# From expert 1 on, w_down is loaded by ScalarE's DMA queue and w_gate_up by SyncE's

## The chip, the core and the metric

The kernel runs on one core of a Trainium2 chip. The core has a matrix engine (TensorE, PE in the profile; its weight loads are PEld), VectorE (DVE), ScalarE (ACT), GpSimd (POOL) and SyncE (SP), each with its own stream of instructions that runs in order. DMA transfers are issued by SP, ACT or POOL and are carried by 16 DMA engines. The metric is the device time of one execution in microseconds, the median of several; less is better.

## The reference

One decoder layer on 512 tokens of 1024 float32 values: three token mixers, an output projection and a layer norm, and then the part that matters here, a routed mixture of 32 experts of which each token uses four:

```python
logits = (xt @ router_w + router_b).astype(F32)
top_val, top_idx = lax.top_k(logits, TOP_K)          # 4 of 32
gate = jax.nn.softmax(top_val, axis=-1)
...
gu = xb @ w_gu[e] + b_gu[e]                          # w_gu[e]: 1024 x 2048
glu = jnp.minimum(gu[:, :D_FF], SWIGLU_LIMIT)
lin = jnp.clip(gu[:, D_FF:], -SWIGLU_LIMIT, SWIGLU_LIMIT)
act = glu * jax.nn.sigmoid(SWIGLU_ALPHA * glu) * (lin + 1.0)
return act @ w_dn[e] + b_dn[e]                       # w_dn[e]: 1024 x 1024
```

The expert outputs are weighted with the gates, summed for each token, added to the layer's input and normalised. All weights are float32: 8 MB of w_gate_up and 4 MB of w_down for each expert, 403 MB (384 x 1 MB) in all.

## The kernel before

The mixers run first (until about 400 us); the experts follow, one after the other, in `experts` (L1348). What belongs to expert e is called g for w_gate_up and d for w_down in this section.

**Chunks and the ring.** Weights come in chunks of 1 MB, 128 partitions by 8 KB: eight chunks g.0 to g.7 for an expert (`load_gu`, L1175), each 128 rows of w_gate_up, and four chunks d.0 to d.3 (`load_dn`, L1183), each 256 rows of w_down. `chunk` (L1165) hands out slots of a ring of 18 in the order of the calls, so a chunk may be loaded when the chunk 18 calls earlier has been read by PE. `load` (L1170) issues the transfer. Before, all are issued by SyncE (`nc.sync`), so all go through one queue, q1 in the profile. Each of the eight DMA semaphores (DMAHW0 to DMAHW7 in the order's rows) is given to every eighth of these transfers, and an issue first waits until the semaphore's earlier transfer is in: no transfer goes out before the one eight places earlier has landed.

**An expert on PE.** At most 96 rows of an expert are done here. The low 64 rows always run: `gu_low` (L1264), per chunk g.k eight matmul records of L1268. The rows 65 to 96 are the optional half, `gu_high` (L1270, L1273), in two blocks of four chunks behind a branch on the expert's count of rows (`past64`, L1257); experts 0 and 31 run it without a branch. `swiglu` (L1275) works on DVE and ACT; `swiglu_T` (L1288) transposes its result on PE (L1295) and ACT copies it to the tile aT, of which there is one. `dn` (L1299) multiplies with w_down: low rows L1314, optional rows L1309 behind a branch. ACT evacuates (L1318: eo0 and eo1) and POOL scatters the rows with an accumulating DMA (L1319). In the loop, after the fourth chunk of an expert the loads of the next expert's w_gate_up and of its own w_down are called, its xg rows for two experts on are gathered by POOL (L1193), and the next expert's rows are transposed (L1207, copies L1208). `dn` of an expert runs behind the w_gate_up products of the next one. The instructions of each engine stand in an order that a scheduler chooses from these calls and from its own estimate of when each can run; it is fixed when the program is built.

**The tail.** `tail` (L1512) adds the last expert's rows by matmuls, and normalises.

Of the kernel before, what the change touches and what calls it, by code (L numbers as in the profile page):

```python
# [126 lines left out]
class Trunk:  # L127
# [1039 lines left out]
        self.nchunk += 1  # L1167
        return self.slot(tag, "wc", dt)[:, 0:2048], self.ring_ins if self.nchunk <= FIRST and tag != "r" else None

    def load(self, dst, src, gate):  # L1170
        i = self.nc.sync.dma_start(dst, src)
        if gate is not None:
            self.after(i, gate)

# [8 lines left out]
    def load_dn(self, e):  # L1183
        out = []
        for k in range(0, NK, 2):
            w, gate = self.chunk()
            self.load(w.rearrange("p (k c) -> p k c", k=2), self.a["w_down"][e, k * 128:(k + 2) * 128].rearrange("(p k) c -> p k c", k=2), gate)
            out += [w[:, 0:1024], w[:, 1024:2048]]
        return out

# [489 lines left out]
```

## Time and profile before

| | us |
|---|---|
| median of 3 runs | 1492.03 (1488.74 to 1493.71) |
| the profiled execution | 1492.41 |
| its span, first to last instruction | 1490.7 |
| first transfer of an expert's weights issued | 294 |
| expert 31: first and last w_gate_up product | 1408.47, 1431.4 |
| last w_down product | 1454.2 |

The profile records one execution. Its views: the page (busy shares, forty slices of the span, queues), busy time by stretch, who waited for whom, and time lines of single engines. A start in a time line is in us from the span's start; "x8" is a run of eight equal instructions and the second number is how long the run took. A busy PE is not a PE at its peak, since matmuls are pipelined and their ends are modelled.

### The profile page before, as it was taken

The numbers are of one execution on the slowest core, as the hardware profiler recorded it, in microseconds if no ns is written. First come the engines' busy times: TensorE is split into PE (matmuls) and PEld (weight loads), VectorE is DVE, ScalarE is ACT, GpSimd is POOL, SyncE is SP. The second block draws the span as 40 slices with busy tenths as digits, with TensorE's granted clock in tenths as the row PEclk, the third lists the DMA queues.
The fourth block names the chain that finished last, engine by engine and source line by source line (L and its number), as shares of the span: only waits on it lengthen the run. The fifth ranks groups of instructions, "written<-read, shape, count | busy, mean of one in ns | idle before, by whom it ended". The sixth has DMA issues, their size and how long they took to land. (4 is left out here: it accounts for less than half of the span.)

```text
span 1490.7 us, 19988 instructions
## 1 busy us (share of the span) xinstructions
PE 1345.4 (90%) x7852; PEld 639.2 (43%) x7853; DVE 466.6 (31%) x1108; ACT 290.7 (20%) x611; POOL 228.2 (15%) x206
## 2 busy tenths in 40 slices
PE   7899989998899999988799999999879888899993
PEld 5677888876533433232233333333323222333322
DVE  4867497697831212111111111111111110211115
ACT  4444243353211111111001111111100110111103
POOL 1111137142301010001001111011100100010111
PEclk9999888799899999999999999999999999999996
DMA  7222123355689999999999999999999999999964
GB/s 250 70 57 71 36 68 89 118 159 205 256 341 396 393 383 404 402 398 390 395 399 398 394 398 399 402 395 391 392 387 398 395 401 394 404 396 412 401 223 127
DMA packets 95232, 461.67 MB, mean 310 GB/s; under 512 B 18137, under 2 KB 26745, under 8 KB 45962
## 3 DMA queue, kind: packets, MB, share of 16 engines
q1 hardware_dynamic: 79674, 434.57, 74.1%
q0 software_dynamic: 10880, 21.32, 6.6%
q10 hardware_dynamic: 4560, 4.15, 0.9%
q8 instruction: 82, 1.34, 0.4%
q14 instruction: 36, 0.29, 0.1%
HBM read 445.97 MB, written 18.10 MB: 311 GB/s over the span
## 5 line engine op out<-in xcount | busy, mean ns | idle before, releaser
L1268 PE MATMUL gu<-wc,xT 128*64 128x512 f32 x2048 | 486.6, 606 | 67.0 <-DMA wc<-w_gate_up 64.4
L1268 PEld LDWEIGHTS gu<-wc,xT 128*64 128x64 f32 x2048 | 143.0, 138 | 392.9 <-issue 239.5
L1281 DVE TENSOR_SCALAR glu<-gu 128x256 f32<-128x256 f32 (+1 forms) x64 | 35.6, 556 | 843.8 <-PE gu L1273 391.5
L1314 PE MATMUL dn<-wc,aT 128*64 128x512 f32 x1024 | 247.6, 603 | 4.2 <-PEq L1261 2.4
L1282 ACT ACTIVATE glu<-glu 128x256 f32<-128x256 f32 (+1 forms) x64 | 33.6, 525 | 549.6 <-DVE glu L1281 549.4
L1193 POOL DMA_INDIRECT xg<-hd,gidx x31 | 31.3, 1009 | 665.0 <-PE tr L1207 659.7
L1314 PEld LDWEIGHTS dn<-wc,aT 128*64 128x64 f32 x1024 | 65.8, 136 | 117.6 <-issue 101.3
L1319 POOL DMA_INDIRECT yd<-eo,sidx x45 | 70.1, 1557 | 276.1 <-ACT eo L1318 276.1
L1273 PE MATMUL gu<-wc,xT 128*32 128x512 f32 x960 | 111.3, 596 | 0.0
L222 PE MATMUL pi<-xhi,whi 128*128 128x512 f32 x152 | 63.7, 419 | 8.9 <-ACT whi L172 8.9
L1208 ACT ACTIVATE xT<-tr 128x384 f32<-128x384 f32 x62 | 29.9, 490 | 177.2 <-PE tr L1207 177.2
L223 PE MATMUL pi<-xlo,whi 128*128 128x512 f32 x152 | 62.8, 413 | 0.6 <-DVE xlo L173 0.6
L1273 PEld LDWEIGHTS gu<-wc,xT 128*32 128x32 f32 x960 | 27.7, 109 | 79.3 <-issue 79.3
L224 PE MATMUL pi<-xhi,wlo 128*128 128x512 f32 x152 | 61.7, 406 | 0.0
L173 POOL TENSOR_TENSOR wlo<-wraw,whi 128x512 fp32r<-128x512 f32 (+1 forms) x28 | 39.3, 1407 | 134.9 <-ACT whi L172 129.4
L1318 ACT ACTIVATE eo<-dn,gate 128x512 f32<-128x512 f32 (+1 forms) x45 | 28.0, 621 | 162.9 <-PE dn L1314 84.4
L1309 PE MATMUL dn<-wc,aT 128*32 128x256 f32 x960 | 56.1, 381 | 1.0 <-ACT aT L1296 1.0
L172 ACT ACTIVATE whi<-wraw 128x512 fp32r<-128x512 f32 (+1 forms) x54 | 33.9, 631 | 56.4 <-DMA wraw<-w_in 25.3
L1309 PEld LDWEIGHTS dn<-wc,aT 128*32 128x32 f32 x960 | 29.5, 110 | 33.3 <-issue 13.8
L1284 DVE SCALAR_TENSOR_TENSOR glu<-glu 128x256 f32<-128x256 f32 (+1 forms) x64 | 35.6, 556 | 8.4 <-ACT glu L1282 7.1
L1295 PEld LDWEIGHTS tr<-ident,glu 128*128 128x128 f32 x192 | 25.7, 208 | 28.0 <-DVE sel L1214 19.5
L222 PEld LDWEIGHTS pi<-xhi,whi 128*128 128x128 f32 x152 | 29.5, 194 | 18.2 <-ACT whi L172 8.6
(489 smaller groups left out, 1585.8 us busy)
## 6 DMA issues: line engine op xcount, KB each, us to landing
wc<-w_gate_up SPq DMA_DIRECT2D x256, 1024.0 KB
wc<-w_down SPq DMA_DIRECT2D x128, 1024.0 KB
wraw<-w_in SPq DMA_DIRECT2D x46, 256.0 KB
wraw<-w_out SPq DMA_DIRECT2D x16, 256.0 KB
xraw<-xT SPq DMA_DIRECT2D x4, 512.0 KB
res<-x SPq DMA_DIRECT2D x4, 512.0 KB
hd<-res ACTq DMA_DIRECT2D x4, 512.0 KB
res<-yd POOLq DMA_DIRECT2D x4, 512.0 KB
```

The source lines that it names most:

```text
L172: self.hi_ins = nc.scalar.activation(hi, src, AF.Copy)
L173: return (eng or nc.vector).tensor_tensor(lo, src, hi, OP.subtract)
L222: nc.tensor.matmul(p, hi, xh, start=(k == 0), stop=False)
L223: nc.tensor.matmul(p, hi, xl, start=False, stop=False)
L224: nc.tensor.matmul(p, lo, xh, start=False, stop=(k == NK - 1))
L1268: mm(p[q][64 * h:64 * h + 64], xT[:, k, 0:64], w[:, 1024 * q + 512 * h:1024 * q + 512 * h + 512], start=False, stop=(k == NK - 1))
L1273: self.nc.tensor.matmul(p[2][32 * c:32 * c + 32], xT[:, k, 64:96], w4[:, c], start=False, stop=(k == NK - 1), skip_group_check=True)
L1281: nc.vector.tensor_scalar(out[:, c], g, 7.0, None, OP.min)
L1284: nc.vector.scalar_tensor_tensor(out[:, c], ln[:, c], 1.0, out[:, c], OP.add, OP.mult)
L1309: mm(p2[32 * c:32 * c + 32], aT[:, 4 + k % 2, 32 * (k // 2):32 * (k // 2) + 32], wd[k][:, 256 * c:256 * c + 256], start=(k == 0), stop=(k ...
L1314: mm(p0[64 * h:64 * h + 64], aT[:, k % 4, 64 * (k // 4):64 * (k // 4) + 64], wd[k][:, 512 * h:512 * h + 512], start=(k == 0), stop=(k == N ...
L1319: return nc.gpsimd.indirect_dma_start(out=self.yd.rearrange("t (c f) -> (t c) f", f=w), out_offset=bass.IndirectOffsetOnAxis(ap=self.sidx[ ...
```

## The change

`load` takes the issuing engine as an argument, and `load_dn` hands it ScalarE for every expert but 0. So 124 of the 384 transfers are issued by ACT's stream, between its activations, and go through ACT's queue (q10). Slots, sizes and semaphores stay as they are; the eight semaphores now go round over the transfers of both queues in the order that the scheduler gave them.

```diff
-    def load(self, dst, src, gate):
-        i = self.nc.sync.dma_start(dst, src)
+    def load(self, dst, src, gate, eng=None):
+        i = (eng or self.nc.sync).dma_start(dst, src)
...
-            self.load(w.rearrange("p (k c) -> p k c", k=2), self.a["w_down"][e, k * 128:(k + 2) * 128].rearrange("(p k) c -> p k c", k=2), gate)
+            self.load(w.rearrange("p (k c) -> p k c", k=2), self.a["w_down"][e, k * 128:(k + 2) * 128].rearrange("(p k) c -> p k c", k=2), gate, self.nc.scalar if e else None)
```

The change also moves the scheduler's order. ACT in the middle, before, one round: sigmoids of expert 27 (glu_9063), transposed rows of expert 29 (xT_9213), outputs of expert 26 (eo0_9091, eo1_9127), transposed result of expert 27 (aT_9130):

```order
L1282 ACTIVATE glu_9063<-glu_9063 128x256
L1282 ACTIVATE glu_9063<-glu_9063 128x512
L1208 ACTIVATE xT_9213<-tr_9214 128x384
L1208 ACTIVATE xT_9213<-tr_9220 128x384
L1261 COMPARE_AND_BRANCH
L1318 ACTIVATE eo1_9127<-dn2_3901,gate_3575 128x256
L1261 UNCONDITIONAL_BRANCH x2
L1318 ACTIVATE eo0_9091<-dn0_9074,gate_3575 128x512
L1296 ACTIVATE aT_9130<-tr_9131 128x512
L1296 ACTIVATE aT_9130<-tr_9137 128x256
```

After, the round that begins behind aT_9130. wc_9204, wc_9206 and wc_9208 are d.1, d.2 and d.3 of expert 28, wc_9003 is d.0 of expert 27, which PE reads behind expert 28's w_gate_up, and eo1_9326 is expert 27's output:

```order
L1171 DMA wc_9204<-w_down 128x2048
L1171 DMA wc_9003<-w_down 128x2048
L1208 ACTIVATE xT_9213<-tr_9214 128x384
L1208 ACTIVATE xT_9213<-tr_9220 128x384
L1261 COMPARE_AND_BRANCH
L1261 UNCONDITIONAL_BRANCH x2
L1171 DMA wc_9206<-w_down 128x2048
L1261 COMPARE_AND_BRANCH
L1318 ACTIVATE eo1_9326<-dn2_3901,gate_3575 128x256
L1261 UNCONDITIONAL_BRANCH x2
L1171 DMA wc_9208<-w_down 128x2048
```

Behind these come the sigmoids of expert 28, eo0 of 27 and the aT copies of 28. Four issues now stand between ACT's copies and sigmoids, wc_9003 behind wc_9204; by the slot that it takes, wc_9204 waits for PE's products with g.3 of expert 28. The copies to xT_9213 have moved from ahead of aT_9130 to behind it.

SyncE at the end, before: g.4 to g.7 of expert 31 (wc_9592 to wc_9598), d.0 to d.3 of expert 30 (wc_9600 to wc_9606), the first of expert 31 (wc_9774; wc_9776, wc_9778 and wc_9780 follow), with the semaphores that each waits for:

```order
L1171 DMA wc_9592<-w_gate_up 128x2048 [waits DMAHW5_49,PE_49]
L1171 DMA wc_9594<-w_gate_up 128x2048 [waits DMAHW6_49,PE_49]
L1171 DMA wc_9596<-w_gate_up 128x2048 [waits DMAHW7_49,PE_49]
L1171 DMA wc_9598<-w_gate_up 128x2048 [waits DMAHW0_49,PE_49]
L1171 DMA wc_9600<-w_down 128x2048 [waits DMAHW1_49]
L1171 DMA wc_9602<-w_down 128x2048 [waits DMAHW2_49,PE_49]
L1171 DMA wc_9604<-w_down 128x2048 [waits DMAHW3_49,PE_49]
L1171 DMA wc_9606<-w_down 128x2048 [waits DMAHW4_49,PE_49]
L1171 DMA wc_9774<-w_down 128x2048 [waits DMAHW5_49,PE_49]
```

SyncE there after; nothing follows of the weights:

```order
L1171 DMA wc_9590<-w_gate_up 128x2048 [waits DMAHW7_49,PE_49]
L1171 DMA wc_9592<-w_gate_up 128x2048 [waits DMAHW1_49,PE_49]
L1171 DMA wc_9594<-w_gate_up 128x2048 [waits DMAHW3_49,PE_49]
L1171 DMA wc_9596<-w_gate_up 128x2048 [waits DMAHW6_49,DMAHW5_49,PE_49]
L1171 DMA wc_9598<-w_gate_up 128x2048 [waits DMAHW6_49,DMAHW0_49,PE_49]
```

ACT there after, behind its issue of wc_9606 (aT_9724 and glu_9657 are expert 30's, xT_9608 is 31's):

```order
L1208 ACTIVATE xT_9608<-tr_9609 128x384
L1208 ACTIVATE xT_9608<-tr_9615 128x384
L1282 ACTIVATE glu_9657<-glu_9657 128x512
L1282 ACTIVATE glu_9657<-glu_9657 128x256
L1171 DMA wc_9776<-w_down 128x2048
L1318 ACTIVATE eo0_9685<-dn0_9668,gate_3575 128x512
L1296 ACTIVATE aT_9724<-tr_9725 128x512
L1296 ACTIVATE aT_9724<-tr_9731 128x256
L1171 DMA wc_9778<-w_down 128x2048
L1171 DMA wc_9780<-w_down 128x2048
L1171 DMA wc_9600<-w_down 128x2048
L1171 DMA wc_9774<-w_down 128x2048
```

The eight w_down chunks that stood behind wc_9598 are now on ACT, and in the order over both engines all but wc_9600 and wc_9774 stand ahead of wc_9598, which by its semaphore waits for wc_9606.

PE at the end, before: low and optional products (gu2) of g.6 and g.7 of expert 31 in turn, then w_down of expert 30 and the transposes:

```order
L1268 MATMUL gu0_9735<-wc_9596,xT_9608 64x512 x2
L1268 MATMUL gu1_9736<-wc_9596,xT_9608 64x512 x2
L1273 MATMUL gu2_9737<-wc_9596,xT_9608 32x512 x4
L1268 MATMUL gu0_9735<-wc_9598,xT_9608 64x512 x2
L1268 MATMUL gu1_9736<-wc_9598,xT_9608 64x512 x2
L1273 MATMUL gu2_9737<-wc_9598,xT_9608 32x512 x4
L1314 MATMUL dn0_9850<-wc_9600,aT_9724 64x512 x3
L1295 MATMUL tr_9840<-ident_60,glu_9814 128x128 x4
L1314 MATMUL dn0_9850<-wc_9600,aT_9724 64x512
L1295 MATMUL tr_9846<-ident_60,glu_9814 128x128 x2
```

After:

```order
L1268 MATMUL gu0_9735<-wc_9596,xT_9608 64x512 x2
L1268 MATMUL gu1_9736<-wc_9596,xT_9608 64x512 x2
L1268 MATMUL gu0_9735<-wc_9598,xT_9608 64x512 x2
L1268 MATMUL gu1_9736<-wc_9598,xT_9608 64x512 x2
L1273 MATMUL gu2_9737<-wc_9592,xT_9608 32x512 x4
L1273 MATMUL gu2_9737<-wc_9594,xT_9608 32x512 x4
L1273 MATMUL gu2_9737<-wc_9596,xT_9608 32x512 x4
L1273 MATMUL gu2_9737<-wc_9598,xT_9608 32x512 x4
L1295 MATMUL tr_9840<-ident_60,glu_9814 128x128 x4
L1314 MATMUL dn0_9850<-wc_9600,aT_9724 64x512 x3
```

The optional products of g.4 to g.7 have moved behind the last low product.

## Rows read from the trace of the kernel before

**Rows 1.** the page: span, PE, the forty slices' GB/s (37.3 us each), queues.

```profile
span 1490.7 us, 19988 instructions
...
PE 1345.4 (90%) x7852; PEld 639.2 (43%) x7853; DVE 466.6 (31%) x1108; ACT 290.7 (20%) x611; POOL 228.2 (15%) x206
...
GB/s 250 70 57 71 36 68 89 118 159 205 256 341 396 393 383 404 402 398 390 395 399 398 394 398 399 402 395 391 392 387 398 395 401 394 404 396 412 401 223 127
...
q1 hardware_dynamic: 79674, 434.57, 74.1%
...
q10 hardware_dynamic: 4560, 4.15, 0.9%
```

**Rows 2.** busy time by stretch: engines, granted TensorE clock, DMA share, GB/s.

```profile
core 0: us, PE busy (x) PEld busy (x) DVE busy (x) ACT busy (x) POOL busy (x), PEclk, DMA share, GB/s
...
800.00:900.00 100.00, 99.64 (x668) 35.90 (x668) 12.66 (x30) 12.30 (x25) 12.36 (x9) 1.00 1.02 393
...
1200.00:1300.00 100.00, 86.43 (x407) 27.61 (x406) 12.88 (x30) 10.45 (x21) 7.72 (x6) 0.97 1.02 397
1300.00:1400.00 100.00, 98.13 (x610) 34.69 (x608) 12.44 (x27) 11.39 (x23) 8.74 (x6) 1.00 1.02 403
sum 950.00, PE 879.61 PEld 304.41 DVE 127.74 ACT 107.64 POOL 92.72; mean PE 109.95 PEld 38.05 DVE 15.97 ACT 13.46 POOL 11.59
```

**Rows 3.** who waited for what, SyncE's DMA queue, 460 to 1400: us, times, longest.

```profile
SPq L1171 <- DMA wc<-w_gate_up: 542.7, 215, 5.2
...
SPq L1171 <- PE gu L1268: 28.2, 13, 10.3
```

**Rows 4.** the same for PE.

```profile
PE gu L1268 <- DMA wc<-w_gate_up: 64.4, 75, 2.9
```

**Rows 5.** time line of PE, two experts: start, us, operation, count.

```profile
568.66 0.49 PE L1207 MATMUL tr<-ident,xg 96*128 96x96 f32 x4
...
570.96 0.55 PE L1207 MATMUL tr<-ident,xg 96*128 96x96 f32 x4
...
814.66 3.64 PE L1273 MATMUL gu<-wc,xT 128*32 128x512 f32 x32
818.23 7.09 PE L1268 MATMUL gu<-wc,xT 128*64 128x512 f32 x32
```

**Rows 6.** SyncE's issues around 930 us, and their durations (ns min/median/max).

```profile
918.67 17.86 SPq L1171 DMA_DIRECT2D wc<-w_gate_up  x8
938.68 9.44 SPq L1171 DMA_DIRECT2D wc<-w_down  x4
...
L1171 SPq DMA_DIRECT2D wc<-w_down x112: 327/328/328, 475.4 to 1381.8; - x112
```

**Rows 7.** DMA rates from 900 to 960 us, forty slices of 1.5 us.

```profile
GB/s 415 437 410 399 369 287 391 404 376 374 337 343 384 421 415 415 437 421 426 415 431 431 415 431 404 431 404 431 393 325 350 403 348 343 397 426 426 410 426 431
DMA packets 3785, 23.90 MB, mean 398 GB/s; under 512 B 513, under 2 KB 641, under 8 KB 1005
```

**Rows 8.** SyncE's issues at the end.

```profile
1384.24 19.64 SPq L1171 DMA_DIRECT2D wc<-w_gate_up  x8
1405.98 19.64 SPq L1171 DMA_DIRECT2D wc<-w_down  x8
```

**Rows 9.** POOL's queue at the end.

```profile
1442.87 1.55 POOL L1319 DMA_INDIRECT yd<-eo,sidx  x1 [31.04 <-ACT eo L1318]
1448.17 0.94 POOL L1507 DMA_DIRECT2D res<-yd  x1 [3.75 <-DMA yd<-eo,sidx]
```

**Rows 10.** time line of PE, expert 31's last low product and what follows.

```profile
1428.46 1.94 PE L1268 MATMUL gu<-wc,xT 128*64 128x512 f32 x8
1430.33 1.07 PE L1273 MATMUL gu<-wc,xT 128*32 128x512 f32 x8
...
1433.86 1.07 PE L1314 MATMUL dn<-wc,aT 128*64 128x512 f32 x2
1434.87 0.50 PE L1295 MATMUL tr<-ident,glu 128*128 128x128 f32 x2
```

## The prediction

> **What bounds the kernel now.** I read the page first, the forty slices and the queues [rows 1]: PE is busy 90% of the span, but from the 13th slice to the 38th (447 to 1416 us, 26 x 37.27 = 969 us) the core moves 383 to 412 GB/s without a gap, nearly all of it on q1, SyncE's queue. Then the stretches [rows 2]: in each the DMA share is 1.02, while PE is busy anywhere from 86 to 99.6 us of 100, so it is not PE that sets the pace. Then who waits for whom. Each issue of SyncE waits for the semaphore of an earlier transfer 215 times where that one brought w_gate_up, 542.7 us in all, and for a matmul that frees a ring slot only 13 times for 28.2 us [rows 3]: slots are nearly always free in time. PE itself waits for w_gate_up in 75 places, 64.4 us [rows 4]. So from about 447 us the transfers set the end, PE follows a few microseconds behind, and ACT, 10 to 12 us busy of 100 [rows 2], is nearly idle.
>
> How much has PE to spare? The transfers take 12 chunks x 2.76 us = 33.1 us for an expert (seven intervals from 1405.98 to the start of the last at 1425.30 [rows 8], which is 19.64 us less one issue of 0.33 [rows 6], so 19.31 / 7 = 2.76). PE is busy 109.95 us of the mean stretch of 118.75 (950 / 8) [rows 2], so it has 7.4% of 33.1 = 2.4 us for each expert, on the mean.
>
> **The change part by part.** *Bytes, instructions, issue cost.* The same 384 chunks of 1 MB are loaded into the same slots. 124 issues leave SyncE and go to ACT, 4 for each expert at 0.328 us [rows 6], so 1.3 us of ACT per 33 us. ACT is busy 10.5 to 12.3 us of 100 [rows 2], its idle time hides it: nothing. If that cover were gone it would be 31 x 1.3 = 40 us.
>
> *The rate.* The stage is bound by what the DMA engines move, and no row shows two hardware queues with 1 MB chunks at once. Below zero: in 21 of the 40 slices from 900 to 960 us the core moves 410 to 437 GB/s, in 11 it moves 287 to 384, with a mean of 398 [rows 7]. If a second queue closed all those dips to 431, 969 x (1 - 398/431) = 74 us would go. Above zero: the stretches between 393 and 403 GB/s [rows 2] show that 1.3% comes and goes with the mixture, 12 us either way. I take 0: the 393 and the 403 are within this, and nothing in them speaks for either sign.
>
> *Order of arrival, in the middle.* Before, one queue brings w_gate_up of expert e+1 and then w_down of e, as PE reads them. After, three of the four w_down chunks travel among w_gate_up, and one of them, the first that PE's w_down product reads, comes late: from expert 17 on ACT issues it behind the next expert's second chunk, and that one waits for PE to have read the fourth w_gate_up chunk of the expert then running (the order's rows for expert 28 in the part on the change). From there to its use PE has four w_gate_up chunks (7.09 us for 32 matmuls) and eight transposes (1.04), so 8.1 us of cover, and 11.8 where the optional half (3.64) runs [rows 5]. How long does a chunk on ACT's queue take to land? At most what SyncE's take, 20.0 us: the chunk issued at 918.67 has to be in before the issue at 938.68, eight later, can go [rows 6]. At least one interval of 2.5 to 2.8 us. A POOL transfer issued at 1442.87, with SyncE's last chunks (20 us from 1425.30) still under way, released its reader at 1448.17, 5.3 us later [rows 9]; so a transfer on another queue doesn't stand behind SyncE's. Two chunks that share the engines half and half with SyncE's need about 2 x 2 x 2.76 = 11.0 us: 2.9 us more than the cover where the optional half doesn't run, none where it does. Over half of the experts that is about 1.5 us each on the mean of all, inside the 2.4 us that PE has to spare: nothing, as long as the engines keep full. The Trainium skill, in "DMA: Bandwidth & Descriptors", section "Queues, rings and completion order", has each DMA engine go round its queue rows packet by packet. [Rows 9] agree; with it the stall is the 1.5 us just given, without it up to 11.9 us for each expert, which is the first rival.
>
> *Do the engines keep full?* Eight semaphores go round over both queues, so SyncE can't get more than seven issues past a chunk that ACT hasn't issued. In the middle that leaves some nine chunks (25 us) from the landing of the fourth w_gate_up chunk to an empty queue, against PE's lag of a few microseconds: 0.
>
> *The end.* Here the order costs, because nothing comes after. Before, w_gate_up of expert 31 is followed by eight w_down chunks, and its last chunk was in by 1425.30 (the issue eight later, [rows 8]); PE's last low product starts at 1428.46 [rows 10]. After, only wc_9600 and wc_9774, the last two of ACT, are behind it in the program's order; six chunks have moved ahead of it. The stream sets the pace, so six places are 6 x 2.76 = 16.6 us. Two of the six (wc_9778, wc_9780) are issued only behind the aT copies and share the engines with SyncE's last, so a chunk or so of these may fall behind: three to six, I take five, since both are issued before wc_9598 can be: 13.8 us. Behind that chunk PE now has four optional products in a row, 3.64 us [rows 5] where it had one of 1.07 [rows 10]: +2.6. It no longer comes 3.2 us late (1425.30 to 1428.46): -3.2. The last two transposes wait for the clamps and sigmoids behind these products; two w_down products that fill this wait before (1.07 us at 1433.86, ahead of the transposes at 1434.87 [rows 10]) are no longer there: +1.0. From there on, w_down of 30 and 31 and the tail are the same work: 0. Sum: 13.8 + 2.6 - 3.2 + 1.0 = +14.2 us, between +8.7 (three places) and +17.0 (six).
>
> The profiled execution took 1492.41 us, its span 1490.7, and is 0.4 us above the median of 1492.03; so 1492.03 + 14.2 = 1506.
>
> **The rivals.** *A. PE is held by the late chunk.* If chunks of ACT's queue land nearly as late as SyncE's, say 16 us, the w_down product waits 16 - 8.1 = 7.9 us in the half without the optional products and 4.2 in the others, 6.0 on the mean, less 2.4 to spare: 3.6 us for each of the 15 experts from 17 on, 54 us, and with the end 1492 + 14 + 54 = 1560; at 13 us it is 3.1 less 2.4, 0.7 us each and 1517. For it: 20.0 us in [rows 6], and the sigmoid and aT copies stand on ACT behind issues that wait. Against: [rows 9]. It decides from some 12.5 us of landing on.
>
> *B. Nothing is changed.* The engines move the same bytes at the same rate; if SyncE's last w_gate_up chunks run ahead of ACT's because ACT issues its last four late, expert 31 is not held, and the time is 1488 to 1498. The Trainium skill says so in "DMA: Bandwidth & Descriptors", section "Issuing engines are not separate DMA queues": two issuers share the same 16 engines and only issue time is saved. [Rows 1] agree in that the stage is full on one queue; what the rule doesn't treat is the order of arrival, on which my sum rests.
>
> *C. Faster.* The second queue fills the dips of [rows 7]. A third of the 74 us would be 25, less the 14 of the end: 1481. For it: dips down to 287 GB/s on a queue that always has work. Against: PE is busy 98.1 and 99.6 of 100 us in two stretches [rows 2] and couldn't follow everywhere.
>
> **How the numbers follow.** The forecast, 1499 to 1514, has 0.50; A, 1515 to 1565, 0.15; B, 1488 to 1498, 0.20; C, 1465 to 1487, 0.15. The range leaves out the outer parts of A (0.09) and C (0.11): 1482 to 1535. A measurement of this kernel can tell 0.3% (4.5 us) from no change: under 1487.6 is faster, 0.15; up to 1496.5 the same, 0.20; above, slower, 0.65.
>
> **What would show it.** Right: the stretches from 450 to 1400 keep a DMA share of 1.0 and 393 to 403 GB/s, q1 carries 434.57 - 130.02 = 304.5 MB and q10 134.2 MB (124 chunks of 1.0486 MB more than [rows 1]), PE's expert 31 has waits for w_gate_up in its last four chunks, and its last low product starts 10 to 17 us later than 1428.46. A would show as PE or its loads waiting for w_down in the middle, over 50 us; C as stretches above 405 GB/s. The forecast is wrong if the middle stretches are longer or shorter by over 1%, or if expert 31's chunks land at 1425 as before.

## The result and the profile after

The changed kernel takes 1525.88 us (median of 4 runs, 1525.51 to 1526.15), the kernel before 1491.47 us in the same session. The ratio is 1.0231 with an interval of 1.0214 to 1.0249, so 34.4 us slower at 1491.47, where +14.2 were forecast. The profiled execution took 1525.90 us, its span is 1524.1. Below, differences are (ratio - 1) x 1491 us, with the ratio that the runs of each kernel gave against the kernel before.

The page of the changed kernel: span, the forty slices (38.1 us each), the two queues.

```profile
span 1524.1 us, 20002 instructions
...
GB/s 245 68 56 69 53 74 107 120 142 259 225 393 392 371 391 399 407 387 385 391 397 398 387 388 394 376 378 339 399 393 394 383 392 397 403 355 394 373 114 128
...
q1 hardware_dynamic: 61818, 304.53, 51.5%
q10 hardware_dynamic: 22416, 134.18, 22.7%
```

The bytes went where the diff says (304.53 MB on SyncE's queue, 134.18 on ACT's), against [rows 1]. But the slices are no longer full: 339 and 355 GB/s stand in the 28th and 36th, where before nothing is under 383.

Busy time by stretch, columns as in [rows 2]:

```profile
core 0: us, PE busy (x) PEld busy (x) DVE busy (x) ACT busy (x) POOL busy (x), PEclk, DMA share, GB/s
...
800.00:900.00 100.00, 99.85 (x682) 38.47 (x680) 13.94 (x30) 11.38 (x24) 13.15 (x10) 1.00 1.02 393
...
1000.00:1100.00 100.00, 87.39 (x504) 32.74 (x502) 13.04 (x28) 9.37 (x20) 9.26 (x7) 0.93 0.97 369
...
1300.00:1400.00 100.00, 93.16 (x570) 33.44 (x570) 12.30 (x28) 9.42 (x21) 9.24 (x7) 0.97 0.99 383
```

From 800 to 900 us nothing differs from [rows 2]. From 1000 to 1100 the DMA share is under 1, for the first time in the stretches from 450 us on, and TensorE's granted clock, 1.00 or 0.97 in [rows 2], is 0.93.

Who waited for what (us in total, times, longest), first PE, then SyncE's queue, 300 to 1470 us:

```profile
PE dn L1309 <- DMA wc<-w_down: 56.1, 9, 9.5
PE gu L1273 <- DMA wc<-w_gate_up: 16.5, 8, 3.8
PE dn L1314 <- DMA wc<-w_down: 7.0, 3, 5.4
...
PE gu L1268 <- DMA wc<-w_gate_up: 3.5, 3, 2.6
```

```profile
SPq L1171 <- DMA wc<-w_down: 519.4, 70, 19.8
SPq L1171 <- DMA wc<-w_gate_up: 282.1, 71, 14.6
SPq L1171 <- PE gu L1268: 65.2, 32, 9.1
```

In [rows 4] PE waits 75 times for w_gate_up, never long, as an engine does that follows the stream. Now it waits 3.5 + 16.5 = 20.0 us for w_gate_up in all, and 56.1 + 7.0 = 63.1 us in twelve places for w_down, up to 9.5 us each. SyncE waited at most 5.2 us for an earlier transfer of w_gate_up in [rows 3]; now up to 19.8 us for one of w_down. Both say that w_down comes late, and that it holds SyncE. And SyncE waits 65.2 us (61.6 in the window of [rows 3], where it was 28.2) for PE's low products to free a slot, so part of the stream's lateness is set by PE.

One table goes with all runs below. From the traces I took, against the kernel before: how much later the stream of weights is when the weights of three experts are in (the ends of all 8 KB packets, 128 for a chunk, counted in order of time), then of 19, 21, 29 and 31; how much later PE starts the first low product of expert 9 and of 31; and how much longer the span is. "Dry" is the time lost up to 1415 us in which the engines were less than 85% busy, in bins of 1 us; "packets" is by how much the durations of the 8 KB packets of 344 chunks, divided by 16 engines, exceed the 889.5 us of before (the 25th to the 368th chunk in order of time). Dry times hold to within 0.8 us, as the bins begin here or there. Times in us; what a row has at expert 3, up to 6 us, comes from the mixers and stays in it (the 19.8 of the last row is a dry spell of its own). In `e2_dorder` and `e10_dorder_x` part of expert 29's w_down products stands behind the first low product of 31, so PE's last column flatters them, and the span is the measure.

| kernel | stream 3, 19, 21, 29, 31 | PE 9, 31 | span | dry | packets |
|---|---|---|---|---|---|
| changed | -2.4, 5.7, 13.7, 18.2, 19.7 | 21.9, 33.6 | 33.4 | 11.0 | 8.7 |
| e1_chain | -2.8, 12.9, 13.2, 18.3, 18.1 | 13.5, 21.5 | 18.9 | 9.3 | 11.2 |
| e2_dorder | 1.1, 11.2, 11.6, 14.6, 14.8 | 13.1, 8.6 | 13.1 | 11.8 | 3.1 |
| e3_early | 3.3, 8.3, 9.3, 7.4, 7.2 | 28.3, 5.6 | 5.3 | 2.9 | 1.9 |
| e4_late | -1.0, 2.3, 6.2, 12.9, 13.7 | -1.4, 28.3 | 26.9 | 10.0 | 3.4 |
| e5_chain_x | 1.5, 10.0, 11.2, 12.1, 12.8 | 13.0, 13.5 | 10.5 | 2.7 | 8.7 |
| e6_one_x | -0.4, -1.1, -1.5, -1.5, -1.4 | -1.3, -1.3 | -2.1 | 0.2 | -0.7 |
| e7_end | -5.5, -5.5, -6.1, -6.5, -1.5 | -6.3, 9.5 | 7.6 | 0.7 | 1.6 |
| e8_after_x | -0.3, 9.3, 16.1, 23.4, 24.6 | 25.0, 40.2 | 37.0 | 12.4 | 9.5 |
| e9_mid | -1.7, 6.0, 14.2, 19.2, 19.2 | 23.0, 28.1 | 27.7 | 11.7 | 7.4 |
| e10_dorder_x | 0.9, 6.9, 8.6, 9.4, 9.2 | 14.1, 2.6 | 10.2 | 2.7 | 6.7 |
| e11_allact_x | 19.8, 29.2, 29.2, 30.4, 34.0 | 18.2, 28.8 | 26.3 | 24.0 | 2.3 |

In the changed kernel everything is lost before expert 31 begins: PE comes to it 33.6 us late and ends 33.4 late. Of the 33.6, 19.7 are the stream, and 13.9 are PE being further behind the stream than before. That divides by place, not by cause. PE's own time divides it too: from expert 3's first low product to the last w_down product, before, changed, and, for later, the run `e10_dorder_x` (columns as in [rows 2]):

```profile
494.98:1454.20 959.22, 887.93 (x5054) 303.20 (x5054) 127.51 (x293) 106.61 (x215) 97.55 (x76) 0.99 1.01 390
```

```profile
491.68:1487.00 995.32, 903.25 (x5054) 330.51 (x5054) 135.08 (x293) 103.50 (x217) 97.12 (x76) 0.96 0.98 376
```

```profile
494.36:1462.88 968.52, 907.35 (x5060) 326.81 (x5060) 162.45 (x349) 81.48 (x161) 97.95 (x76) 0.97 1.00 387
```

For the same 5054 matmul records the changed kernel takes 36.1 us more: 15.3 in which PE is busy, at a granted clock of 0.96 against 0.99, and 20.8 in which it is idle.

### The profile page after: what moved, and what is told of

Read it like the earlier page. It is cut to its first block, busy times and chain, and to the rows that moved or that the text cites. A ratio compares the mean times of both kernels' runs of the same rounds, so it can differ in the third digit from the quotient of the medians.

```text
span 1524.1 us, 20002 instructions
## 1 busy us (share of the span) xinstructions
PE 1355.4 (89%) x7852; PEld 662.2 (43%) x7853; DVE 473.5 (31%) x1108; ACT 287.3 (19%) x611; POOL 228.7 (15%) x206
## 3 DMA queue, kind: packets, MB, share of 16 engines
q1 hardware_dynamic: 61818, 304.53, 51.5%
q10 hardware_dynamic: 22416, 134.18, 22.7%
## 5 line engine op out<-in xcount | busy, mean ns | idle before, releaser
L1268 PE MATMUL gu<-wc,xT 128*64 128x512 f32 x2048 | 503.2, 599 | 12.5 <-PEq L1261 6.9
L1268 PEld LDWEIGHTS gu<-wc,xT 128*64 128x64 f32 x2048 | 153.6, 137 | 314.9 <-issue 294.6
L1281 DVE TENSOR_SCALAR glu<-gu 128x256 f32<-128x256 f32 (+1 forms) x64 | 35.7, 558 | 687.9 <-PE gu L1273 266.4
L1314 PE MATMUL dn<-wc,aT 128*64 128x512 f32 x1024 | 236.3, 597 | 7.2 <-DMA wc<-w_down 7.0
L1314 PEld LDWEIGHTS dn<-wc,aT 128*64 128x64 f32 x1024 | 77.5, 138 | 151.8 <-issue 140.1
L1273 PE MATMUL gu<-wc,xT 128*32 128x512 f32 x960 | 115.0, 611 | 16.6 <-DMA wc<-w_gate_up 16.5
L1309 PE MATMUL dn<-wc,aT 128*32 128x256 f32 x960 | 71.9, 462 | 57.1 <-DMA wc<-w_down 56.1
L1318 ACT ACTIVATE eo<-dn,gate 128x512 f32<-128x512 f32 (+1 forms) x45 | 27.9, 621 | 486.8 <-PE dn L1309 241.5
L1309 PEld LDWEIGHTS dn<-wc,aT 128*32 128x32 f32 x960 | 38.2, 132 | 94.8 <-issue 81.7
L1208 ACT ACTIVATE xT<-tr 128x384 f32<-128x384 f32 x62 | 27.0, 488 | 255.4 <-PE tr L1207 111.9
L1273 PEld LDWEIGHTS gu<-wc,xT 128*32 128x32 f32 x960 | 27.7, 110 | 95.3 <-issue 66.5
L1282 ACT ACTIVATE glu<-glu 128x512 f32<-128x512 f32 (+1 forms) x64 | 31.6, 520 | 181.3 <-DVE glu L1281 174.8
L1284 DVE SCALAR_TENSOR_TENSOR glu<-glu 128x512 f32<-128x512 f32 (+1 forms) x64 | 34.2, 557 | 65.7 <-ACT glu L1282 59.0
L1213 DVE TENSOR_SCALAR sel<-cst 128x128 fp32r<-128x128 f32 x32 | 8.1, 254 | 123.8 <-PE gu L1246 78.0
L1283 DVE TENSOR_SCALAR glu<-gu 128x256 f32<-128x256 f32 (+1 forms) x64 | 35.4, 553 | 8.8 <-PE gu L1268 8.8
```

The source lines that it names most:

```text
L1268: mm(p[q][64 * h:64 * h + 64], xT[:, k, 0:64], w[:, 1024 * q + 512 * h:1024 * q + 512 * h + 512], start=False, stop=(k == NK - 1))
L1273: self.nc.tensor.matmul(p[2][32 * c:32 * c + 32], xT[:, k, 64:96], w4[:, c], start=False, stop=(k == NK - 1), skip_group_check=True)
L1281: nc.vector.tensor_scalar(out[:, c], g, 7.0, None, OP.min)
L1283: nc.vector.tensor_scalar(ln[:, c], l, 7.0, -7.0, OP.min, OP.max)
L1284: nc.vector.scalar_tensor_tensor(out[:, c], ln[:, c], 1.0, out[:, c], OP.add, OP.mult)
L1309: mm(p2[32 * c:32 * c + 32], aT[:, 4 + k % 2, 32 * (k // 2):32 * (k // 2) + 32], wd[k][:, 256 * c:256 * c + 256], start=(k == 0), stop=(k ...
```

## One stall, read through

How the two are made can be seen around 1018 us. PE of the changed kernel (start, us, operation, count):

```profile
1013.79 0.51 PE L1245 MATMUL gu<-mb,sel 128*128 128x512 f32 x1
1018.08 6.50 PE L1309 MATMUL dn<-wc,aT 128*32 128x256 f32 x64 [3.79 <-DMA wc<-w_down]
1024.52 7.09 PE L1314 MATMUL dn<-wc,aT 128*64 128x512 f32 x32
```

ACT there, its own and its queue's:

```profile
1004.83 6.55 ACTq L1171 DMA_DIRECT2D wc<-w_down  x3
1024.70 0.47 ACT L1318 ACTIVATE eo<-dn,gate 128x256 f32<-128x256 f32 x1 [28.30 <-PE dn L1309]
1024.93 0.33 ACTq L1171 DMA_DIRECT2D wc<-w_down  x1
```

Granted clock and share of two stretches (columns as in [rows 2]), and the rate from 1020 to 1040 us in slices of 0.5 us:

```profile
core 0: us, PE busy (x) PEld busy (x) DVE busy (x) ACT busy (x) POOL busy (x), PEclk, DMA share, GB/s
...
1014.00:1018.00 4.00, 0.29 (x1) 0.00 (x0) 0.36 (x2) 0.00 (x0) 0.00 (x0) 0.88 0.96 342
1018.00:1024.50 6.50, 6.42 (x64) 3.30 (x64) 0.00 (x0) 0.00 (x0) 0.00 (x0) 0.55 1.01 426
```

```profile
GB/s 442 410 426 459 410 393 475 393 442 410 410 492 377 410 164 164 82 279 426 410 377 358 225 127 33 37 20 2 0 131 33 147 360 459 377 377 275 348 336 348
```

At 1004.83 ACT issues d.1 of expert 18 and behind it, at 1005.20, d.0 of expert 17, the one that PE reads next. It lands at 1017.95, 12.75 us later. PE has worked off its cover by 1014.3 and waits 3.8 us. Then it pays twice: the 64 optional products take 6.50 us, where they take 3.64 without a wait ahead of them (at 800.23 us in the same trace), with a granted clock of 0.55, so nearly all of it at the lower of the levels of 1.2 and 2.4 GHz. ACT pays next. Its next issue, d.3 of expert 18, stands behind the output eo1 (L1318), which reads these products. The 28.30 us are ACT's idle time since its last activation; its stream has stood at this output since its third issue ended at 1011.38, so for 13.3 us, and d.3 goes out at 1024.93 and lands at 1033.81. SyncE's next issue waits for just that semaphore: the eight have gone round. From 1032 to 1036 us the engines move 0 to 147 GB/s. So a wait of 3.8 us has become some 4 us of dry engines between 1027 and 1046 us, of the 7.2 us that the stream loses from expert 19 to 20 (5.7 to 12.9 us late).

## Experiments: which part of the program

Four runs undo the change for some experts. The diff is one line, `e3_early`:

```diff
-... gate, self.nc.scalar if e else None)
+... gate, self.nc.scalar if 0 < e < 17 else None)
```

> w_down on ACT's queue for experts 1 to 16 alone, from 17 on SyncE's as before. In the changed kernel the stream of weights is some 5 us behind that of before at expert 17 against expert 2, so the theory (cost comes in single stalls, and most of them after expert 17 and at the end) says 1492 + 3 to 8 = 1495 to 1500 us. Rival (each chunk on the second queue costs the same): 34 x 64 / 124 = 18 us, 1509 us.

Measured: 1494.46 us, ratio 1.0031 (1.0006 to 1.0056), 4.6 us. The cost is not one for each chunk. PE falls 28 us behind by expert 9 (22 in the changed kernel), yet this is nearly all made good: the first low product is 25.8 us late at expert 17 and 5.5 at 23, so 3.4 us for each expert in which nothing holds PE, where the prediction had 2.4 us to spare.

`e4_late` has `if e > 16`:

> w_down on ACT's queue for experts 17 to 31 alone. Theory: 1492 + 34 - 5 = 1521 us, 1512 to 1525, with a dry spell of the DMA engines of some 7 us in the middle. Rival (each chunk costs the same): 34 x 60 / 124 = 16 us, 1508 us.

Measured: 1517.80 us, 1.0194 (1.0137 to 1.0252), 28.9 us, with a dry spell at 1033 to 1038 us. Nearly the same number of chunks as in the early half costs six times as much. Fewer experts are left to make the lag good, and none behind 31; but PE's waits for w_down are also longer here, 33.1 + 7.8 = 40.9 us against 22.8 + 0.9 = 23.7 in `e3_early`, and the end is in it. The two runs don't separate these.

`e7_end` has `if e > 28`, `e9_mid` its complement, `if 0 < e < 29`:

> w_down on ACT's queue for experts 29 to 31 alone, SyncE's for all others: the end by itself. The prediction's term says +14 us, because w_gate_up's last chunk of expert 31 lands behind w_down (1506 us, that chunk in at 1435 to 1442, 10 to 17 us behind the last one of before). The theory of now says 1502 to 1509 us too, but by another way: PE waits for d.0 of expert 29 or 30, comes to expert 31's w_gate_up late and finds all of it there.

> The complement of e7_end: w_down on ACT's queue for experts 1 to 28, on SyncE's for 29 to 31; the first 330 loads stand in the changed kernel's order. Theory (the middle delays the stream of weights by some 20 us, and the end costs its own 13 to 14 because PE comes to expert 31 late): the two add up, so 1492 + 34 - 13.5 = 1512 us, 1505 to 1516. Rival (all is settled at the end, where PE's lag is all that counts, and the middle is made good there): 1492 to 1500 us.

`e7_end`: 1504.57 us, 1.0119 (1.0074 to 1.0164), 17.7 us; by its trace 7.6 + 6.1 = 13.7, for its stream ran 6.1 us early until expert 28. `e9_mid`: 1522.04 us, 1.0223 (1.0182 to 1.0264), 33.2 us. I expected the two to add up to the whole; they don't: the end alone costs 14 to 18, the middle alone 33 (27.7 by its span), both together 34. PE of `e9_mid` over the last 90 us of its weights, columns as in [rows 2]:

```profile
core 0: us, PE busy (x) PEld busy (x) DVE busy (x) ACT busy (x) POOL busy (x), PEclk, DMA share, GB/s
1370.00:1460.00 90.00, 89.40 (x561) 30.65 (x560) 10.55 (x22) 9.55 (x20) 8.33 (x6) 1.00 0.95 378
```

With w_down of 29 to 31 back on SyncE's queue PE is busy 89.4 of 90 us, and still ends 27.7 us late: it came 26.5 us late to expert 29 and then had work without a gap, so nothing could be made good, and little that the end adds could show. In `e7_end`, whose PE comes in time, the end shows:

```profile
1401.28 6.17 PE L1309 MATMUL dn<-wc,aT 128*32 128x256 f32 x64 [2.50 <-DMA wc<-w_down]
...
1417.96 7.09 PE L1268 MATMUL gu<-wc,xT 128*64 128x512 f32 x32
```

PE waits for d.0 of expert 29 until 1401.28, again with slow products behind (6.17 us for 64), and begins expert 31's w_gate_up at 1417.96, 1408.47 before: 9.5 us late, 15.8 against its own early start. Its last w_gate_up chunk is issued at 1417.82, where it was issued at 1403.56 before, and PE doesn't wait for it either; by then two lags of about one size lie over each other, and this run doesn't tell which of them would bind without the other.

## Experiments: what in the change costs

`e2_dorder` keeps ACT's four issues of an expert in order, d.0 first (`self.prev`, here and below, starts as None):

```diff
-        i = (eng or self.nc.sync).dma_start(dst, src)
+        i, p = (eng or self.nc.sync).dma_start(dst, src), self.prev; self.prev = i if eng else p; p and eng and self.after(i, p)
```

> As the changed kernel, but ACT's issues are kept in the order d.0, d.1, d.2, d.3 of each expert; SyncE's loads stay free. Theory A (the first chunk that w_down's product reads, d.0, is issued last and lands late): most of the 34 us comes back, 1490 to 1505 us. Theory B (it is ACT, whose issues stand behind an output that waits for PE, that holds SyncE's semaphores, with d.0 only the place where it shows): the issues now stand ahead of the outputs too, so this run gives the same; a rival without both (two queues move less) says 1520 to 1530 us.

Measured: 1506.30 us, 1.0119 (1.0074 to 1.0165), 17.7 us: about half of the loss goes with the late d.0. PE's waits for w_down in this run, 440 to 1470 us:

```profile
PE dn L1314 <- DMA wc<-w_down: 32.0, 17, 4.8
...
PE dn L1309 <- DMA wc<-w_down: 1.8, 3, 1.2
```

33.8 us instead of 63.1, hardly any of it ahead of the optional products, and the span is 13.1 us longer than before, not 33.4. But this run undoes more than the late issue. The scheduler's order on PE has moved too: the kernel before has most of the low w_down products ahead of the optional ones (24 of 32, whose last 8 open the first rows below), the changed kernel has them behind (at 1018.08 and 1024.52 above), `e2_dorder` ahead again (24 ahead, then the second rows).

```profile
837.50 1.94 PE L1314 MATMUL dn<-wc,aT 128*64 128x512 f32 x8
839.37 3.66 PE L1309 MATMUL dn<-wc,aT 128*32 128x256 f32 x64
842.96 1.94 PE L1314 MATMUL dn<-wc,aT 128*64 128x512 f32 x8
```

```profile
1020.27 3.66 PE L1309 MATMUL dn<-wc,aT 128*32 128x256 f32 x64
1023.87 1.94 PE L1314 MATMUL dn<-wc,aT 128*64 128x512 f32 x8
```

What d.0's place on ACT and what PE's order are worth by themselves, no run shows. The dry spells stay, 11.8 us. The longest, ACT and its queue, and the rate from 955 to 985 us in slices of 0.75 us:

```profile
956.82 0.87 ACT L1296 ACTIVATE aT<-tr 128x512 f32<-128x512 f32 x2
968.77 0.49 ACT L1208 ACTIVATE xT<-tr 128x384 f32<-128x384 f32 x1 [11.08 <-PE tr L1207]
968.83 2.39 ACTq L1171 DMA_DIRECT2D wc<-w_down  x4
```

```profile
GB/s 415 448 415 426 393 404 393 306 429 325 317 254 128 63 68 55 33 22 33 87 87 360 502 360 453 410 371 355 350 415 393 437 437 393 437 404 426 437 393 470
```

Here it is not d.0 or the output: the four issues at 968.83 stand behind the copy of the next expert's transposed rows (L1208), for which ACT waits 11.08 us for PE, while all but one of the transfers ahead have landed (the last two at 966.77 and 969.45). So theory A holds for half, theory B for another part, by another activation than I had named.

`e10_dorder_x` has the copies made by VectorE besides, `e8_after_x` only that:

```diff
-            nc.scalar.activation(xT[:, 4 * q:4 * q + 4], p[:, :4 * CAP].rearrange("p (k t) -> p k t", k=4), AF.Copy)
+            nc.vector.tensor_copy(xT[:, 4 * q:4 * q + 4], p[:, :4 * CAP].rearrange("p (k t) -> p k t", k=4))
```

> e2_dorder (d.0 first on ACT) with the copies of the transposed rows by VectorE, so that neither the late d.0 nor these copies hold anything. Theory: the dry spells of e2_dorder (11.8 us) fall under 4, and 1506 becomes 1494 to 1501 us; what is left over 1492 is the rate on two queues and the end. Rival (the order of SyncE's loads among ACT's costs by itself): 1503 to 1508 us.

> The changed kernel with the copies of the transposed rows (L1208) by VectorE, the loads in the same order. There d.0 is still the last of its expert to be issued, and d.3 still stands behind an output that waits for PE. Theory: these two remain, 1514 to 1526 us, PE's waits for w_down over 35 us. If the copies are what holds ACT here too: 1500 to 1510 us.

`e10_dorder_x`: 1501.31 us, 1.0067 (1.0045 to 1.0089), 10.0 us, dry spells down to 2.7 us; just above the upper edge of what the theory expected. `e8_after_x`: 1530.59 us, 1.0282 (1.0241 to 1.0324), no gain at all and 5 us over the range that I gave; in the changed kernel's own order the copies are not what holds ACT. Moving them helps only once the late d.0 is out of the way.

In `e10_dorder_x` a span 10.2 us longer is left, with a stream 9.2 us late at expert 31. Is that the price of two queues? `e1_chain` orders every load behind the one called before it, so that the loads stand in the order of the kernel before, on two queues; `e5_chain_x` has the copies by VectorE too; `e6_one_x` is that on SyncE's queue alone, `e11_allact_x` on ACT's from expert 2 on. The diff of `e1_chain`:

```diff
-        i = (eng or self.nc.sync).dma_start(dst, src)
+        i, p = (eng or self.nc.sync).dma_start(dst, src), self.prev; self.prev = i; p and self.after(i, p)
```

`e6_one_x` has `self.nc.scalar if e else None` taken out besides, `e11_allact_x` adds `self.nc.scalar if e > 1 else None` to the load of w_gate_up.

> w_down still on ACT's queue, w_gate_up on SyncE's, but every weight load is ordered behind the one called before it, so that the program's order of the loads is that of the kernel before (w_gate_up of e+1, then d.0 to d.3 of e, ACT's four issues ahead of the outputs of the expert before). Theory (the order in which w_down arrives, and ACT's issues that stand behind activations waiting for PE, cost the time; a second queue in itself costs nothing): 1487 to 1500 us, PE's waits for w_down in the middle under 10 us where the changed kernel has 63, no dry spell of the DMA engines. Rival (two queues of 1 MB chunks move less than one, whatever the order): over 1515 us.

> As e1_chain, but the copies of the transposed rows (L1208), behind which ACT's four issues of w_down stand there, are made by VectorE. In e1_chain they wait for PE's transposes, ACT's issues go out up to 10 us late, and the engines run dry for 9.3 us in all. Theory (what ACT waits for ahead of its issues is what empties the queues): dry spells under 3 us, and 1512 falls to 1494 to 1503 us. Rival (two queues move less than one): 1508 to 1515 us, the dry spells gone or not.

> The control of e5_chain_x: the same order of all loads and the same copies by VectorE, but one queue, SyncE's. Both theories: 1488 to 1497 us, as the kernel before; if the copies by VectorE themselves gain or lose, it shows here.

> The order of all loads of e5_chain_x and e6_one_x, copies by VectorE, but from expert 2 on every load is issued by ACT: one queue, held by what ACT waits for. Two claims are tested by it. The packets of 8 KB took longer on the engines in e5_chain_x than in e6_one_x (in all 898 us against 889 for 344 chunks); if that is two queues at once, it is 887 to 891 us here. And if issues behind ACT's waits empty the queue, this has the longest dry spells of all, over 15 us, and a time over 1515 us; if ACT can be held without harm, 1488 to 1497 us.

Measured: `e1_chain` 1512.05 us, 1.0164 (1.0111 to 1.0216), 24.5 us; `e5_chain_x` 1504.87, 1.0107 (1.0072 to 1.0141), 16.0; `e6_one_x` 1490.37, 1.0022 (1.0001 to 1.0043), 3.3; `e11_allact_x` 1516.66, 1.0167 (1.0131 to 1.0203), 24.9. `e1_chain` went against me: the order of before does not bring the time of before. Part of it is again ACT's hold (dry 9.3 us, gone in `e5_chain_x`, 2.7). The rest remains with no dry spell. Two stretches of `e5_chain_x`, then of its control `e6_one_x`, columns as in [rows 2]:

```profile
450.00:600.00 150.00, 141.53 (x752) 53.48 (x749) 25.60 (x55) 13.10 (x26) 16.01 (x12) 0.95 1.01 389
...
1200.00:1300.00 100.00, 85.18 (x399) 29.07 (x397) 16.45 (x36) 7.49 (x15) 7.71 (x6) 0.93 1.01 393
```

```profile
450.00:600.00 150.00, 144.89 (x798) 55.93 (x795) 29.23 (x65) 13.64 (x27) 17.04 (x13) 1.00 1.02 398
...
1200.00:1300.00 100.00, 83.42 (x405) 26.70 (x404) 16.26 (x36) 7.49 (x15) 7.71 (x6) 1.00 1.02 397
```

The share is 1.01 in the one and 1.02 in the other, but 389 and 393 GB/s against 398 and 397. TensorE's granted clock differs as well, 0.95 and 0.93 against 1.00, and no run holds one of the two while the other changes. The packets last longer (898.2 us in sum against 888.8). `e11_allact_x` has one queue and 891.8: a little over the 887 to 891 that I had set for "it is two queues at once", so most of the 9 us of packet time goes with the two queues, and a third may go with issues that come late. The runs don't show by what way, and it varies (3.1 us in `e2_dorder`, 11.2 in `e1_chain`). The hold itself shows most plainly in `e11_allact_x`, ACT with its queue, and the rate from 460 to 500 us in slices of 1 us:

```profile
461.52 0.33 ACTq L1171 DMA_DIRECT2D wc<-w_gate_up  x1
480.79 0.60 ACT L1296 ACTIVATE aT<-tr 128x512 f32<-128x512 f32 x1 [18.80 <-PE tr L1295]
480.97 0.34 ACTq L1171 DMA_DIRECT2D wc<-w_gate_up  x1
```

```profile
GB/s 426 401 426 365 287 365 371 346 227 83 30 0 0 0 0 16 0 0 0 0 0 41 123 410 451 426 418 385 361 299 324 332 410 418 401 418 418 442 426 410
```

ACT issues at 461.52, then waits 18.80 us in the copies of aT (L1296) for PE's transposes, and the engines move next to nothing from 470 to 481 us.

## Why the prediction was wrong, point by point

**What bounds the kernel** was read rightly: the stream of weights, with PE close behind. Issue cost: nothing; ACT is busy 9.4 to 11.4 us of 100 in the stretches above.

**The middle was the step that failed: "inside the 2.4 us that PE has to spare: nothing".** The landing was sized well. A chunk of ACT's queue landed 11.3 us after its issue (median of 106 chunks; 11.0 was the estimate), SyncE's some 15, where before they took 22.3; so a transfer of the second queue doesn't stand behind the first's. The Trainium skill, in "DMA: Bandwidth & Descriptors", section "Queues, rings and completion order", has each engine go round its queue rows, and the medians agree. [Rows 9], on which I had rested this, don't show it: by the 20 us that I gave a chunk, SyncE's last one was in by 1445.3, ahead of the 1448.17 at which POOL's transfer released its reader. But the late d.0 took 13.1 us on the median of 28 experts and 8.8 to 23.8, and I priced a mean stall against a mean spare. Stalls come whole: twelve waits make 63.1 us, four of them at experts ahead of 17, from which on I had looked for them (8.48 us at 502.09 is the first), and behind the longer ones the optional products run slower. Their line on the page, first of the changed kernel, then of `e6_one_x`, where no wait for w_down stands ahead of them:

```profile
L1309 PE MATMUL dn<-wc,aT 128*32 128x256 f32 x960 | 71.9, 462 | 57.1 <-DMA wc<-w_down 56.1
```

```profile
L1309 PE MATMUL dn<-wc,aT 128*32 128x256 f32 x960 | 56.1, 381 | 1.0 <-ACT aT L1296 1.0
```

71.9 us against 56.1 for the same 960 products, so 15.8 us more, about all that PE's busy time has grown by. Against that, the 3.4 us that PE makes good in an expert without a stall are too little where twelve of 28 stall. This is rival A, which had 0.15: 63 us of waits for w_down (over 50 were said to mark it) and a time between 1515 and 1565. It was priced by a landing of 16 us for all experts from 17 on; a landing of 13, which gave 1517 by A's own sum, was enough with its wide spread, since I hadn't priced the clock. That 1525.88 lies within 1482 to 1535 is rival A's doing, not that of the forecast's sum.

**"Do the engines keep full? ... 0"** failed too: 11.0 us dry. The nine chunks of reserve were counted from PE's read of one chunk, as if ACT were free. It stands behind an output or a copy that waits for PE, 13.3 us in the stall shown, and by the eight semaphores SyncE stands behind ACT.

**"The rate ... I take 0"**: packets took 8.7 us more, inside the +12 that I gave as the upper bound. The Trainium skill's rule, in "DMA: Bandwidth & Descriptors", section "Issuing engines are not separate DMA queues", which was rival B, says that two issuers save issue time only; the trace agrees that nothing is saved, and adds that something may be lost.

**The end: right in size, wrong in what it means for the sum.** +14.2 was forecast, 13.7 (by its trace) to 17.7 measured alone. That the size agrees is in part luck: in `e7_end` PE came late by d.0 of expert 29 and waited for no chunk of expert 31's w_gate_up. In the changed kernel it adds 1 us by the medians and 6 by the spans (33.4 against the 27.7 of `e9_mid`), because PE comes to the end with a lag as large. The last chunk of w_gate_up was not what PE waited for. PE there, and ACT:

```profile
1429.67 5.52 PE L1309 MATMUL dn<-wc,aT 128*32 128x256 f32 x64 [4.95 <-DMA wc<-w_down]
1435.12 7.09 PE L1314 MATMUL dn<-wc,aT 128*64 128x512 f32 x32
1442.04 1.02 PE L1268 MATMUL gu<-wc,xT 128*64 128x512 f32 x2
...
1461.88 3.64 PE L1273 MATMUL gu<-wc,xT 128*32 128x512 f32 x32
```

```profile
1406.73 15.08 ACTq L1171 DMA_DIRECT2D wc<-w_down  x4
1435.31 0.47 ACT L1318 ACTIVATE eo<-dn,gate 128x256 f32<-128x256 f32 x1 [28.49 <-PE dn L1309]
```

PE waits for d.0 of expert 29 until 1429.67 and starts expert 31 at 1442.04, 33.6 us late (1408.47 before). ACT again stands at eo1 for the optional products, from 1421.81, where its fourth issue ends, to 1435.31. From 1442.04 on PE has no wait for a transfer; the optional block ends at 1465.5, not 1431.4.

The sum of the parts, from run to run: the late d.0, with PE's order, 16.7 us (34.4 to 17.7), the copies that hold ACT's issues 7.7 (17.7 to 10.0), and 10.0 left; by the spans 20.3, 2.9 and 10.2. Both differences are uncertain by some 7 us, by the interval of `e2_dorder`. The cause of what is left stays open. Longer packets (6.7) and dry spells (2.7) would fill it, by the table. But by the rows of PE's own time in the first section, `e10_dorder_x` has PE idle 10.1 us less than before and busy 19.4 us more, at a granted clock of 0.97 against 0.99, so a slower PE is a rival that no run rules out. No version was faster than the kernel before.

## What to carry to other kernels

A DMA that is issued from a computing engine is as late as the last activation ahead of it, and where semaphores go round over two queues, the other queue is as late as that. Before loads are moved to such an engine, look what it waits for ahead of each issue, and which chunk of a block is read first. And weigh a stall not against mean spare time but against what is left of the program to make it good: stalls of the first half cost 5 us here, those of the second, longer and with the end among them, 29; costs of two places that delay the same engine don't add.

## What the runs showed of the hardware that was not expected

Behind the wait shown above TensorE's granted clock was 0.55 (1018.0 to 1024.5 us, after a stretch with 0.29 us busy of 4), so that a wait of 3.8 us cost 2.9 us more than itself (6.50 against 3.64 us for 64 products). The 64 products behind the seven waits of 4.9 to 9.5 us ahead of such products took 5.06 to 6.42 us; behind a wait of 2.44 us at 984.07 they took 3.66. Packets of 8 KB from two hardware queues took 0.3 to 1.3% longer in sum than from SyncE's alone (892.6 to 900.7 us against 889.5, in the kernels with all of w_down on ACT's queue, one trace each); ACT's queue alone took 891.8, so the lower end of this is no more than one queue can show, and the way of it stays open.
